# Layer 1 of a hybrid trunk: two heads' queries and keys ahead of the values, a latent-attention head ahead of the differential ones

## Chip, cores and metric

One core of one Trainium2 chip. The metric is the device time of one execution in microseconds (us), the median of several runs; lower is better.

## What is computed

Two layers of one trunk. 256 context tokens and 256 latent tokens of width 1024 share each layer's weights. In each layer the normalised tokens go through one input projection whose columns feed three groups of heads: A, differential attention (4 heads, two softmaxes a head); B, latent attention with low-rank keys and values (4 heads); C, a two-way RWKV-7 recurrence (4 heads, a 64 by 64 state). An output projection, a gated MLP with a width-3 convolution, and residuals follow. Only the latent stream is returned, so layer 1 computes attention outputs for latent tokens alone, which still read the context's keys and values. The part that matters here, cut from the reference:

```python
q1, q2, k1, k2, v = diff_qkv(pa, ang_a)                  # group A, latent tokens
K1 = jnp.concatenate([ck1, k1], axis=1)                  # context keys, then latent keys
V = jnp.concatenate([cv, v], axis=1)
oa = over_query_blocks(lambda a_, b_: diff_attn(a_, b_, K1, K2, V, lam), q1, q2)
qb, kb, vb = mla_qkv(pb, P, ang_b)                       # group B
ob = over_query_blocks(lambda q_: softmax_attn(q_, Kb, Vb), qb)
ocr, S_f, S_b = rwkv7_mix(pcr, zero, zero, P, ctx_out)   # group C, context
orr, _, _ = rwkv7_mix(pr, S_f, S_b, P, True)             # group C, latents, from the context's state

def diff_attn(q1, q2, k1, k2, v, lam):
    p1 = softmax32(jnp.einsum('bqhd,bkhd->bhqk', q1, k1) * scale)
    p2 = softmax32(jnp.einsum('bqhd,bkhd->bhqk', q2, k2) * scale)
    return jnp.einsum('bhqk,bkhe->bqhe', (p1 - lam * p2), v)
```

## The kernel before

Every projection is done with three matmuls for each 128-row piece of the contraction (`mm3`, L276 to L279): weights and activations are split into a high part and a rest. The weights' split is made on chip by `wgroup` (L261): a DMA on SyncE's queue brings 512 KB (`wr..`), ScalarE rounds it to the high part (`wh..`, L269), VectorE takes the difference (`wl..`, L270). In the mixing stage there are 3 buffers for the raw weights, 3 for the high part and 4 for the rest.

The change is in the mixing stage of layer 1, for the latent tokens. `attention` (called with `PLAN1`, L141) writes its steps from a string, one word a step: `b`/`B` the latent-attention projection, `qN` keys and query of differential head N (`diff_project`, L1082: 24 matmuls of 256 columns each for keys and query, then the rotary operation `rope`, L876, on VectorE), `v` the values of all four differential heads for all 512 tokens (`diff_v`, L1048: four weight groups, 96 matmuls of 512 columns into the four PSUM tiles `acc`, then four ScalarE copies, L1059), `pN` queries and keys of latent-attention head N (`prepare`, L988), `yN` latent-attention head N (`head`, L1008), `lN` differential head N, `a` a column chunk of the modulation, `g`/`h` the ends of head pairs. `sN` lets the recurrence's generator (`rwkv_seq`) go N steps further. The recurrence first makes masked scores (matmuls L643 to L646 into PSUM tag `r`, two buffers; VectorE masks each by L648), then inverts a unit triangular matrix by 31 elimination steps on VectorE (a transposition L682, then L695 and L697 in turn, closed by the transposition L700), whose result TensorE uses at L717 and L726; then four steps of the recurrence proper, one for each 64 tokens (L753 to L816).

The words only give the order in which the program is written. A scheduler of the framework then sets each engine's order from the dependencies and its own estimates, and each engine works that order strictly off: what stands behind a waiting instruction waits too. The scheduler may therefore let values' matmuls run between the scores and may move splits of weights far ahead.

## Time and profile before

| | us |
|---|---|
| three timed runs | 1359.21, 1366.96, 1369.14 |
| their median | 1366.96 |
| the profiled execution | 1361.95 |
| its span, first to last instruction | 1360.1 |

Over the whole span TensorE is busy 95%, VectorE 71%, ScalarE 51% and GpSimd 2%; TensorE's mean granted clock is 0.981 of full speed. A busy TensorE is not one at its peak: matmuls are pipelined and the ends shown are modelled, so the starts of successive matmuls tell their price. Busy shares are means over stages with different limits; the rows below are therefore of the stage that is changed, from about 970 to 1130 us of the span.

### The profile page before, as it was taken

How to read it: one execution, taken by the hardware profiler on the slowest of the kernel's cores; microseconds unless marked ns; L12 is line 12 of the kernel's file. 1: busy time of each engine (PE TensorE's matmuls, PEld its weight loads, DVE VectorE, ACT ScalarE, POOL GpSimd, SP SyncE). 2: the span in 40 equal slices, each digit the busy share in tenths (PEclk: the TensorE clock that was granted, in tenths of full speed). 3: DMA queues.
4: the chain of work that ended last, by engine and by line, in shares of the span. 5: the costliest groups of instructions: out<-in, count | busy, mean ns of one | idle time of the engine just before them, and what ended most of it. 6: DMA issues, size and time to landing. Idle time of an engine off the chain costs nothing.

```text
span 1360.1 us, 27958 instructions
## 1 busy us (share of the span) xinstructions
PE 1285.8 (95%) x11208; PEld 1079.1 (79%) x11208; DVE 965.8 (71%) x2438; ACT 696.1 (51%) x1368; POOL 21.1 (2%) x41
## 2 busy tenths in 40 slices
PE   5999999998989999999999999999998997999997
PEld 4787766665777888999999888889865775999996
DVE  3548667657679587866769579587869587777776
ACT  4335244765664554534446555655545654555553
POOL 0001000000000000000000000000100000000000
PEclk9999899997999999999999999999998998999999
DMA  9830265300886565432557446447220048456662
GB/s 323 273 108 16 62 178 183 116 1 2 299 283 189 168 218 170 130 118 78 163 184 224 140 152 206 138 122 214 63 63 1 2 138 265 140 170 202 186 183 81
DMA packets 216531, 202.50 MB, mean 149 GB/s; under 512 B 7825, under 2 KB 175313, under 8 KB 216401
## 3 DMA queue, kind: packets, MB, share of 16 engines
q1 hardware_dynamic: 216400, 200.71, 47.6%
q8 instruction: 88, 1.44, 0.4%
q14 instruction: 43, 0.34, 0.1%
HBM read 198.55 MB, written 2.13 MB: 148 GB/s over the span
## 4 chain that ended last, share of the span: by engine, by line
PE 79%; DVE 13%; ACT 4%; issue 2%; DMA 1%; SPq 0%; POOL 0%; ACTq 0%; DVEq 0%; POOLq 0%
PE g L277 10%; PE g L279 10%; PE g L278 10%; PE acc L277 7%; PE acc L279 7%; PE acc L278 7%; PE r L277 3%; PE r L279 3%; PE r L278 3%; PE acc L906 3%; PE g L1103 2%; PE acc L902 1%; PE r L770 1%; PE r L789 1%; PE acc L322 1%
## 5 line engine op out<-in xcount | busy, mean ns | idle before, releaser
L270 DVE TENSOR_TENSOR wlf<-wrf,whf 128x1024 fp32r<-128x1024 f32 x176 | 214.3, 1220 | 58.8 <-ACT whf L269 37.2
L269 ACT ACTIVATE whf<-wrf 128x1024 fp32r<-128x1024 f32 x176 | 184.6, 1051 | 31.2 <-DMA wrf<-in_ffn_w_up_dram 8.6
L277 PE MATMUL g<-hl,whf 128*128 128x256 f32 x528 | 149.7, 285 | 0.9 <-DVE gv L458 0.8
L278 PE MATMUL g<-hl,whf 128*128 128x256 f32 x528 | 148.9, 284 | 0.0
L279 PE MATMUL g<-hl,wlf 128*128 128x256 f32 x528 | 147.0, 284 | 0.1
L454 ACT ACTIVATE gv<-g,pers 128x256 f32<-128x256 f32 x110 | 61.9, 563 | 155.6 <-PE g L279 154.6
L277 PEld LDWEIGHTS g<-hl,whf 128*128 128x128 f32 x528 | 100.9, 191 | 4.8 <-issue 2.2
L278 PEld LDWEIGHTS g<-hl,whf 128*128 128x128 f32 x528 | 101.0, 191 | 1.9 <-issue 0.3
L277 PE MATMUL g<-hc,whf 128*128 128x256 f32 x352 | 100.6, 286 | 1.6 <-DVE gv L458 0.9
L278 PE MATMUL g<-hc,whf 128*128 128x256 f32 x352 | 100.4, 285 | 0.0
L279 PEld LDWEIGHTS g<-hl,wlf 128*128 128x128 f32 x528 | 99.7, 191 | 1.0 <-issue 0.3
L279 PE MATMUL g<-hc,wlf 128*128 128x256 f32 x352 | 100.0, 285 | 0.0
L457 DVE SCALAR_TENSOR_TENSOR gv<-g,pers,gv 128x255 f32<-128x255 f32 x110 | 52.7, 479 | 65.5 <-ACT gv L454 65.5
L270 DVE TENSOR_TENSOR wlm<-wrm,whm 128x1024 fp32r<-128x1024 f32 (+2 forms) x64 | 71.9, 1132 | 33.3 <-ACT whm L269 19.6
L277 PE MATMUL acc<-whf,at 128*128 128x512 f32 x220 | 87.9, 402 | 0.4 <-ACT ar L344 0.4
L278 PE MATMUL acc<-wlf,at 128*128 128x512 f32 x220 | 87.5, 398 | 0.6 <-DVE wlf L270 0.6
L279 PE MATMUL acc<-whf,at 128*128 128x512 f32 x220 | 86.8, 395 | 0.1
L269 ACT ACTIVATE whm<-wrm 128x1024 fp32r<-128x1024 f32 (+2 forms) x64 | 62.5, 987 | 38.8 <-PE acc L279 17.4
L277 PEld LDWEIGHTS g<-hc,whf 128*128 128x128 f32 x352 | 67.2, 191 | 4.5 <-issue 2.5
L278 PEld LDWEIGHTS g<-hc,whf 128*128 128x128 f32 x352 | 67.2, 191 | 1.5 <-issue 0.2
L279 PEld LDWEIGHTS g<-hc,wlf 128*128 128x128 f32 x352 | 67.1, 191 | 0.4
L895 ACT ACTIVATE pa<-g,pers 128x512 f32<-128x512 f32 (+1 forms) x72 | 44.2, 615 | 32.9 <-DVE pers L894 32.4
(534 smaller groups left out, 3434.4 us busy)
## 6 DMA issues: line engine op xcount, KB each, us to landing
wrf<-in_ffn_w_up_dram SPq DMA_DIRECT2D x110, 512.0 KB
wra<-in_ada_w_dram SPq DMA_DIRECT2D x80, 512.0 KB
wrf<-in_ffn_w_down_dram SPq DMA_DIRECT2D x66, 512.0 KB
wrm<-in_w_in_dram SPq DMA_DIRECT2D x52, 512.0 KB
wro<-in_w_out_dram SPq DMA_DIRECT2D x24, 512.0 KB
wrs<-in_ada_w_dram SPq DMA_DIRECT2D x32, 256.0 KB
gt<-gate SPq DMA_DIRECT2D x6, 512.0 KB
wrm<-in_w_in_dram SPq DMA_DIRECT2D x8, 352.0 KB
```

Of the source, the lines that this page charges most:

```text
L269: S.activation(h[:, :n], raw[:, :n], AF.Copy)
L270: V.tensor_tensor(lo[:, :n], raw[:, :n], h.bitcast(F32)[:, :n], ALU.subtract)
L277: first = TE.matmul(ps, lh[0], rh[0], start=start, stop=False)
L278: TE.matmul(ps, lh[0], rh[1], start=False, stop=False)
L279: TE.matmul(ps, lh[1], rh[0], start=False, stop=stop)
L322: ins = TE.matmul(ps[q * 32 : q * 32 + 32, :], ca[:, k, :], ws[k // 2][:, c0 : c0 + P], start=k == 0, stop=k == KT - 1)
L454: S.activation(o[:, : n * SQ], ps[:, : n * SQ], AF.Identity, scale=wc, bias=bias)
L457: V.scalar_tensor_tensor(o3[:, :, 1:SQ], p3[:, :, 0 : SQ - 1], wp, o3[:, :, 1:SQ], ALU.mult, ALU.add)
L770: chain[s] = TE.matmul(px[eo * 64 : eo * 64 + 64, pd, :], sc[:, pd, eo, 0:64], SV[:, pd, eo, :], start=True, stop=True)
L895: S.activation(pr_[:, :nk], ps[:, :nk], AF.Exp, bias=m, accum_out=sm)
L906: TE.matmul(po[:, :width], pT[:, b * P : (b + 1) * P], vtiles[b], start=(b == 0), stop=(b == nb - 1))
L1103: ins = TE.matmul(ps[:, :nk], qT[:, i, qc : qc + P], kT_[:, :nk], start=True, stop=True)
```

## The change

Layer 1's plan has keys and query of head 1 (`q1`) ahead of the values (`v`) and not behind them, and the latent-attention head `y0` ahead of the differential heads `l1` and `l0`. So that the scheduler does not draw the values' matmuls forward again, the first matmul of each of the values' four tiles (`mm3` returns the first of its three, and `behind` takes it where `k8 == 0`) gets an edge of order alone, without a semaphore, behind the last matmul written before the values, the last one of `q1`'s query. Layer 0 is not touched.

```diff
-    PLAN1 = "b B s15 q0 v p0 s15 q1 l1 l0 s15 y0 g0 p2 p1 q2 y1 p3 y2 s5 l2 q3 y3 a a s99 h a s20 a l3 a g1"
+    PLAN1 = "b B s15 q0 q1 v p0 s15 y0 l1 l0 s15 g0 p2 p1 q2 y1 p3 y2 s5 l2 q3 y3 a a s99 h a s20 a l3 a g1"
...
+    last_mm = [None]
+
+    def behind(ins, first):
+
+        if first is not None:
+            tc.add_manual_dep(
+                ins.ins, first.ins.name,
+                mybir.DependencyInfo(mybir.DependencyClass.NoSync, mybir.DependencyReason.DATA), reason="issue order",
+            )
...
-        TE.matmul(ps, lh[1], rh[0], start=False, stop=stop)
+        last_mm[0] = TE.matmul(ps, lh[1], rh[0], start=False, stop=stop)
...
         pss = [PS(tag) for _ in js]
+        first = last_mm[0]
...
                     ins = mm3(ps, h.tok(k8, j), (wg[0][:, k, :], wg[1][:, k, :]), k8 == 0, k8 == 7)
+                    if l == 1 and k8 == 0:
+                        behind(ins, first)
```

Lines of the changed kernel stand 10 lower than before from `mm3` on, and 13 lower behind `diff_v`. In the names, `g_1457` and the like are PSUM tiles, `hl` latent and `hc` context activations, `whm`/`wlm` the parts of a weight group; equal weight groups carry other numbers in the two kernels.

First place: TensorE, where the values begin. Before: the last matmuls of head 0's query (`g_1457`), then the values' tile `acc_1459`.

```order
L277 MATMUL g_1457_11032<-hl_1340_10255,whm_1455_11028 128x256
L278 MATMUL g_1457_11032<-hl_1340_10255,whm_1455_11028 128x256
L558 MATMUL r_1421_10781<-pers_63,d4_1420_10778 128x2 x3
L279 MATMUL g_1457_11032<-hl_1340_10255,wlm_1456_11029 128x256
L277 MATMUL acc_1459_11063<-whm_1464_11069,hc_994_7676 128x512
L278 MATMUL acc_1459_11063<-wlm_1465_11070,hc_994_7676 128x512
L279 MATMUL acc_1459_11063<-whm_1464_11069,hc_994_7676 128x512
L277 MATMUL acc_1460_11064<-whm_1464_11069,hc_994_7676 128x512
```

Changed: the last matmuls of head 1's query (`g_1467`), then the values' tile `acc_1469`. Ahead of these rows all four pairs of masked scores and the first half of the transposes L681 to L684 have gone.

```order
L288 MATMUL g_1467_11105<-hl_1340_10255,whm_1465_11101 128x256
L289 MATMUL g_1467_11105<-hl_1340_10255,wlm_1466_11102 128x256
L287 MATMUL g_1467_11105<-hl_1340_10255,whm_1465_11101 128x256
L288 MATMUL g_1467_11105<-hl_1340_10255,whm_1465_11101 128x256
L289 MATMUL g_1467_11105<-hl_1340_10255,wlm_1466_11102 128x256
L287 MATMUL acc_1469_11136<-whm_1474_11142,hc_994_7676 128x512
L288 MATMUL acc_1469_11136<-wlm_1475_11143,hc_994_7676 128x512
L289 MATMUL acc_1469_11136<-whm_1474_11142,hc_994_7676 128x512
```

Before, 74 of the values' 96 matmuls stood between and ahead of the scores and 22 behind the first half of the transposes; in the changed order none stands ahead, and all 96 follow in one piece.

Second place: VectorE and ScalarE, ahead of the elimination. VectorE before: two weight rests (of head 1's query and head 2's keys), the rotary operation of `p0`, and the transposition L682 that opens the elimination; head 1's rotary operation comes within it.

```order
L648 TENSOR_TENSOR d4_1439_10916<-r_1441_10918,pers_63 128x4x128
L270 TENSOR_TENSOR wlm_1499_11459<-wrm_1497_11456,whm_1498_11458 128x1024
L270 TENSOR_TENSOR wlm_1562_11904<-wrm_1560_11901,whm_1561_11903 128x1024
L881 STREAM_SHUFFLE sh_1477_11197<-g_1476_11193 32x256
L884 TENSOR_TENSOR sh_1477_11197<-g_1476_11193,pers_63 32x256
L883 TENSOR_TENSOR sh_1477_11197<-sh_1477_11197,pers_63 32x256
L682 STREAM_TRANSPOSE d4_1482_11243<-d4_1429_10840 128x1024
L889 TENSOR_TENSOR bq_1475_11191<-sh_1477_11197 32x256
```

VectorE changed: `wlm_1484` is the values' fourth group, `wlm_1562` and `wlm_1567` are keys and query of head 2, `wlm_1606` keys of head 3; L692 opens the elimination.

```order
L899 TENSOR_TENSOR bq_1485_11264<-sh_1487_11270 32x256
L270 TENSOR_TENSOR wlm_1484_11233<-wrm_1482_11230,whm_1483_11232 128x1024
L270 TENSOR_TENSOR wlm_1562_11904<-wrm_1560_11901,whm_1561_11903 128x1024
L270 TENSOR_TENSOR wlm_1567_11940<-wrm_1565_11937,whm_1566_11939 128x1024
L270 TENSOR_TENSOR wlm_1606_12205<-wrm_1604_12202,whm_1605_12204 128x1024
L692 STREAM_TRANSPOSE d4_1492_11316<-d4_1429_10840 128x1024
L698 COPY d4_1493_11318<-pers_63 128x16 x2
L904 TENSOR_REDUCE pers_63<-g_1503_11494 128x1
```

The elimination now stands behind the rest of a weight group of head 3, two groups further on than before, and the first instruction inside it is a row maximum of `y0`.

ScalarE at the same place, around the four copies of the values (L1059, in the changed kernel L1072). Before: the copies, and right behind them the high part of head 2's keys (`whm_1561`).

```order
L1059 ACTIVATE va_1016_7741<-acc_1459_11063 128x512
L1059 ACTIVATE va_1016_7741<-acc_1460_11064 128x512
L1059 ACTIVATE va_1017_7742<-acc_1461_11065 128x512
L1059 ACTIVATE va_1017_7742<-acc_1462_11066 128x512
L269 ACTIVATE whm_1561_11903<-wrm_1560_11901 128x1024
L1001 ACTIVATE bq_1475_11191<-g_1476_11193 96x256
```

ScalarE changed: the copies, and right behind them the high part of head 3's keys (`whm_1605`), which `wlm_1606` above waits for.

```order
L269 ACTIVATE whm_1561_11903<-wrm_1560_11901 128x1024
L269 ACTIVATE whm_1566_11939<-wrm_1565_11937 128x1024
L1072 ACTIVATE va_1016_7741<-acc_1469_11136 128x512
L1072 ACTIVATE va_1016_7741<-acc_1470_11137 128x512
L1072 ACTIVATE va_1017_7742<-acc_1471_11138 128x512
L1072 ACTIVATE va_1017_7742<-acc_1472_11139 128x512
L269 ACTIVATE whm_1605_12204<-wrm_1604_12202 128x1024
```

The high parts of head 2's two groups moved ahead of the copies, and head 3's took their place behind them.

Third place: TensorE, ahead of the elimination's first use. Before: the last work of `p1` (L997 to L1004), then L717; head 2's projections (`g_1563`) follow.

```order
L906 MATMUL acc_1550_11845<-vb_1015_7740,pa_1547_11833 128x64 x4
L1004 MATMUL g_1559_11897<-bm_1012_7734,bm_1013_7735 64x512
L717 MATMUL r_1485_11317<-d4_1483_11245,d4_1430_10841 32x32 x8
L717 MATMUL r_1485_11317<-d4_1483_11245,d4_1433_10866 32x32 x8
L717 MATMUL r_1485_11317<-d4_1483_11245,d4_1436_10891 32x32 x8
L717 MATMUL r_1485_11317<-d4_1483_11245,d4_1439_10916 32x32 x8
L277 MATMUL g_1563_11907<-hl_1337_10252,whm_1561_11903 128x256
```

Changed: the last matmuls of head 2's query (`g_1568`) and a score matmul of `y1` stand ahead of that use, which is L727 here.

```order
L287 MATMUL g_1568_11943<-hl_1340_10255,whm_1566_11939 128x256
L288 MATMUL g_1568_11943<-hl_1340_10255,whm_1566_11939 128x256
L289 MATMUL g_1568_11943<-hl_1340_10255,wlm_1567_11940 128x256
L1023 MATMUL g_1571_11975<-bq_1556_11886 128x512
L727 MATMUL r_1495_11390<-d4_1493_11318,d4_1430_10841 32x32 x8
```

Head 2's 48 projection matmuls moved from behind L717 to ahead of it.

## Rows read from the trace of the kernel before

**Rows 1.** Busy time by stage: stretch, length, engines (rows), clock, DMA share, GB/s.

```profile
core 0: us, PE busy (x) PEld busy (x) DVE busy (x) ACT busy (x) POOL busy (x), PEclk, DMA share, GB/s
...
974.88:1008.45 33.57, 33.57 (x302) 25.56 (x302) 24.95 (x59) 14.20 (x29) 0.00 (x0) 1.00 0.29 79
...
1012.70:1048.85 36.15, 29.32 (x144) 18.32 (x143) 34.31 (x122) 17.67 (x46) 0.00 (x0) 0.91 0.00 1
...
1048.85:1094.20 45.35, 45.35 (x640) 33.49 (x639) 27.86 (x74) 29.06 (x77) 1.04 (x2) 1.00 0.01 2
...
1094.20:1130.73 36.53, 30.77 (x182) 23.91 (x182) 29.08 (x104) 22.81 (x46) 0.00 (x0) 0.99 0.64 204
```

**Rows 2.** Timeline, TensorE: start us, us, what, [idle before <-releaser].

```profile
974.88 0.40 PE L277 MATMUL acc<-whm,hc 128*128 128x512 f32 x1
...
980.11 0.39 PE L279 MATMUL acc<-whm,hl 128*128 128x512 f32 x1
...
1008.03 0.39 PE L279 MATMUL acc<-whm,hl 128*128 128x512 f32 x1
...
1011.47 0.39 PE L277 MATMUL g<-hl,whm 128*128 128x256 f32 x1
...
1017.21 0.28 PE L279 MATMUL g<-hl,wlm 128*128 128x256 f32 x1
...
1022.54 6.86 PE L1103 MATMUL g<-qk,qz 128*128 128x512 f32 x10 [5.05 <-DVE qz L889]
```

**Rows 3.** Timeline, ScalarE, after the values' last matmul.

```profile
1006.41 2.64 ACT L1059 ACTIVATE va<-acc 128x512 f32<-128x512 f32 x4 [2.10 <-PE acc L279]
...
1009.08 1.06 ACT L269 ACTIVATE whm<-wrm 128x1024 fp32r<-128x1024 f32 x1
```

**Rows 4.** Timeline, VectorE, around the scores and the elimination.

```profile
980.95 2.35 DVE L270 TENSOR_TENSOR wlm<-wrm,whm 128x1024 fp32r<-128x1024 f32 x2
...
983.22 0.87 DVE L574 SCALAR_TENSOR_TENSOR d<-rk,pers,r 128x256 f32<-128x256 f32 x2
...
990.57 0.68 DVE L624 TENSOR_TENSOR rk<-r,rk 128x512 f32<-128x512 f32 x1
...
1000.69 1.29 DVE L648 TENSOR_TENSOR d<-r,pers 128x512 f32<-128x512 f32 x2 [0.90 <-PE r L644]
...
1010.16 1.23 DVE L270 TENSOR_TENSOR wlm<-wrm,whm 128x1024 fp32r<-128x1024 f32 x1 [7.05 <-ACT whm L269]
...
1012.70 2.09 DVE L682 STREAM_TRANSPOSE d<-d 128x1024 f32<-128x1024 f32 x1
...
1047.81 1.04 DVE L700 STREAM_TRANSPOSE d<-d 128x512 f32<-128x512 f32 x1
```

**Rows 5.** Lines, VectorE, 1012.7 to 1048.85: line, shapes, count | busy us, mean ns.

```profile
L695 DVE TENSOR_TENSOR d<-d,d 128x126 f32<-128x126 f32 (+22 forms) x31 | 7.8, 252 | 0.4
...
L697 DVE TENSOR_TENSOR d<-d,d 128x126 f32<-128x126 f32 (+22 forms) x31 | 7.8, 251 | 0.4
...
L270 DVE TENSOR_TENSOR wlm<-wrm,whm 128x1024 fp32r<-128x1024 f32 x2 | 2.4, 1216 | 0.0
...
L881 DVE STREAM_SHUFFLE sh<-g 128x256 f32<-128x256 f32 (+1 forms) x3 | 1.3, 442 | 0.1
...
L883 DVE TENSOR_TENSOR sh<-sh,pers 128x256 f32<-128x256 f32 (+1 forms) x2 | 0.8, 422 | 0.0
```

**Rows 6.** Timeline, TensorE, the four steps of the recurrence.

```profile
1049.14 1.98 PE L717 MATMUL r<-d,d 32*32 32x32 f32 x64
...
1054.28 0.27 PE L753 MATMUL r<-pers,rk 64*64 64x64 f32 x1
...
1093.73 0.45 PE L816 MATMUL r<-std,d 128*64 128x64 f32 x8
```

**Rows 7.** Lines, TensorE, 1048.85 to 1094.2.

```profile
L277 PE MATMUL g<-hl,whm 128*128 128x256 f32 x17 | 5.3, 311 | 0.0
...
L1124 PE MATMUL acc<-pers,oh 128*128 128x128 f32 x4 | 0.7, 286 | 0.0
```

**Rows 8.** Busy time, 10 us from 1020: columns as in rows 1.

```profile
1020.00:1030.00 10.00, 6.86 (x10) 2.76 (x10) 9.00 (x29) 2.33 (x6) 0.00 (x0) 0.66 0.00 1
```

## The prediction

> **What bounds the kernel now.** I read four views in this order: busy time by stage, the timelines of the three engines through the changed stage, VectorE's and TensorE's costliest lines in two of its stretches, and busy time in slices of 10 us. The reader should see three different limits in one stage.
>
> From 974.88 to 1008.45 TensorE has no gap: 33.57 us busy of 33.57 [rows 1]. The values' matmuls fill whatever time the masked scores leave, and the scores' chain runs on VectorE beside them [rows 4]. So the values cost little beyond their own 96 issues.
>
> From 1012.70 to 1048.85 VectorE is the limit: 34.31 of 36.15 us busy, while TensorE has 29.32 at a granted clock of 0.91 [rows 1]. This is the elimination, from L682 to L700 [rows 4]. Its own 62 operations are only 15.6 us [rows 5]; the rest is other VectorE work that stands between them.
>
> From 1048.85 to 1094.20 TensorE is busy for the whole 45.35 us [rows 1]: the recurrence's four steps take 1054.28 to 1093.73 and a bit, about 39.9 us or 10.0 a step [rows 6], and projections of other heads stand between their links [rows 7].
>
> What joins these is a chain: last value matmul ends at 1008.45, four copies on ScalarE end at 1009.05 [rows 2, 3], the split L269 takes 1.06 behind them [rows 3], VectorE, idle for 7.05 us and waiting for exactly that split, takes the rest L270 at 1010.16 and only then opens the elimination at 1012.70 [rows 4]. The elimination itself needs nothing of the values. It is late because it stands on VectorE behind a weight rest whose high part stands on ScalarE behind the values' copies. The changed order keeps this link (second place in the order above), so the question is when the values end.
>
> **The values' end.** Before, 74 of the 96 lay among the scores; now all 96 come behind the scores, all of head 1's 48 matmuls, and the first transposes. First the scores. The two weight rests at 980.95 (2.35 us) [rows 4] give way to one rotary part of three operations, about 3 x 0.42 = 1.2 [rows 5], so the chain of preparations on VectorE is 1.15 earlier: its last row, which ended at 990.57 + 0.68 = 991.25 [rows 4], ends near 990.1. Behind it VectorE has eight masks (1.29 for two [rows 4], so 0.65 each, 5.2) and three weight rests (1.22 each [rows 5], 3.6), with 0.4 for the first matmul before a mask: 999.3. Then TensorE makes the first transposes, about 1.0 (an estimate: half the 1.98 of L717's 64 matmuls as small as these [rows 6]) and the last eight of the query's matmuls, 8 x 0.12 = 1.0, where 0.12 is (1017.21 - 1011.47) over 47 intervals [rows 2]. With a link of 0.2 the values start near 1001.5. They start 1.5 earlier if those matmuls run beneath the last mask, and 2.7 later if three pairs of masks each wait 0.90 for their matmuls as one did [rows 4].
>
> The values' spacing is (980.11 - 974.88) / 23 = 0.227 us [rows 2], so 96 take 21.8 and end near 1023.3. Copies 0.6, split 1.06, rest 1.22, links 0.2: the elimination opens at 1026.4 instead of 1012.70, **+13.7** (bounds +12.2 and +16.4).
>
> A cross-check by TensorE's work alone: with no gap the stretch would end 48 x 0.12 = 5.8 us later, at 1014.2. That it ends at 1023.3 means some 9 us of gaps among the scores, which the values no longer fill; VectorE's masks and rests set the pace there.
>
> **Inside the elimination.** Out of it go about ten rotary operations (head 1's nine and one of `p0`), 10 x 0.43 = 4.3 [rows 5], and, net, one weight rest, 1.2. Into it come the rotary operations of `p1` and of head 2's keys, eight of 0.42, 3.4, a normalising product and a query's rest of 0.7 each (estimates by the 0.68 of the 512-column row in [rows 4]). Sum **-0.6**: 35.5 us in place of 36.15. The reordering of `y0`, `l1` and `l0` adds and removes no operation; their order within a stretch that VectorE bounds costs nothing as long as TensorE ends first. It should: 29.32 busy at 0.91 is 26.7 us of full clock, head 1's 48 matmuls go out, head 2's 48 come in. The elimination then closes near 1026.4 + 35.5 = 1061.9, **+13.1**.
>
> **After it.** Head 2's 48 matmuls and the four of L1124 (0.66 by their row, 4 x 0.286 = 1.1 if not overlapped [rows 7]) now stand ahead of the first use of the elimination's result: 48 x 0.12 + 0.66 = 6.4 us less in a stretch where TensorE has no gap [rows 1]. They are paid for beneath the elimination, where TensorE waits anyway (5.05 us in one place [rows 2]). What is late next is the recurrence's own links, which these matmuls covered in the first step: TensorE, VectorE and ScalarE hand on five times a step, and VectorE is busy 27.86 of 45.35 and ScalarE 29.06 [rows 1], 61 and 64%. I take 1.4 us of exposed links (about two gaps of the 0.7 that small operations take), so **-5.0**. Bounds: 0, if the links are what takes the 10 us a step, and -6.4. The stretch 1094.20 to 1130.73 [rows 1] has the same instructions in the same order: 0.
>
> Moved DMAs: the weights' loads keep their order with the plan's words, and DMA has a 29% share among the scores and none in the elimination [rows 1], so I cost them at nothing; if one comes late, it is within the +16.4.
>
> Sum: +13.7 - 0.6 - 5.0 = **+8.1**. The profiled execution took 1361.95, so 1370.0; the median of the runs shown is 1366.96, so 1375.1. I do not know which of the two a new series lies nearer to and take the middle of the bases, 1364.5: **1372.5 us**. One per cent, about what a measurement of this kernel can tell from no change, is 13.7 us, so +8 counts as no change.
>
> **Rivals.**
>
> A, everything is given back (other side). TensorE's work is the same in both kernels and it is busy 95% of the span; if the recurrence's steps are limited only by the work between their links, the steps could shrink from 10.0 to 10.0 - 13.1/4 = 6.7 us, the point from which this decides, and the lateness is gone at the end: 1364.5 or slightly below. For it: TensorE is without a gap there, and the last stretch has 36.53 - 30.77 = 5.8 us free [rows 1]. Against: only 6.4 us of work have moved out; the rest of the filling still stands between the links.
>
> B, nothing is given back. A gapless TensorE in that stretch can be modelled ends: the links (TensorE to VectorE to ScalarE and back) take 10 us a step and the projections lie beside them free. Then +13.1: 1377.6. For it: head 2's 48 matmuls at 0.12 are 5.8 us of issue, but the rows call their lines busy 311 ns each [rows 7], so busy time overstates. Against: 640 matmuls in 45.35 us is one per 71 ns, with 48 at 120 among them. The Trainium skill, "Perfetto Trace Analysis", section "Identifying the Most-Contended Engine", says that matmul busy time is a poor measure, since matmuls are pipelined, and that the busy share of weight loads is a better one. By it this stretch is 33.49 / 45.35 = 74% full [rows 1], the moved 6.4 us might have been free, and the time would be B's.
>
> C, the clock. From 1020 to 1030 the granted clock is 0.66 with TensorE busy 6.86 us of 10 [rows 8], after a wait of 5.05 [rows 2]; the levels are 1.2 and 2.4 GHz. If the changed elimination, whose heads wait for VectorE even more often, runs at that clock throughout, TensorE needs (26.7 + 0.7) / 0.66 = 41.5 us where VectorE needs 35.5, and the first use comes 6.0 later: +14.1, 1378.6. It decides from 27.4 / 35.5 = 0.77 downwards. Against: the mean over the whole elimination was 0.91 [rows 1]. The Trainium skill, "TensorE: Matmul & The Clock Gate", Part 1, says the lower clock is the default and that sustained activity releases it; the row agrees in that the fall comes after the wait.
>
> That the change does not do what it says is excluded by the order shown above.
>
> **How the numbers follow.** Forecast 0.56, with a range of its own from 1366 to 1378 (the bounds of the start, of the give-back in part, and the 2.6 us on either side between the two bases); A 0.13, B 0.19, C 0.12. The range reaches from a little below A to a little above C: 1361.5 to 1381.5. Faster by over 1% (below 1353.3) needs A and another 11 us: 0.05. Slower by over 1% (above 1380.6) is half of C, a quarter of B and the upper end of the forecast: 0.20. Within 1%: 0.75.
>
> **What would show it.** In the profile of the changed kernel: the values in one piece from about 1001.5 to 1023.3 with VectorE waiting for ScalarE's split just before the elimination; the elimination's first transposition (L692) near 1026.4, its last near 1061; the first use (L727) within 1 us of it; four steps that end near 1102. If the elimination opens before 1020, or the values start before the masks end, the first step of the sum is wrong. If the first step of the recurrence still takes 10 us or more, the give-back is; if the granted clock in the elimination is below 0.77, C has come.

## The result, and the profile after

The changed kernel takes 1374.05 us (median of 13 runs, 1368.01 to 1385.81) against 1364.83 us for the kernel before, measured again beside it (13 runs, 1359.04 to 1375.47). The ratio is 1.0081, 95% interval 1.0059 to 1.0104: slower by 11 us, or 0.8%, and inside the bound of 1% that the forecast set for "no change", though clear of zero. The profiled execution has a span of 1372.2 us, 12.1 more than before. The one of the changed kernel (1374.04 us) is at its median, the one of before (1361.95) is 2.9 us below that kernel's median, so a part of the 12.1 belongs to the two executions and not to the change.

The stage after, to be read against [rows 1]. The columns are stretch, length, then busy time and instructions of TensorE, its weight loads, VectorE, ScalarE and GpSimd, the granted clock, DMA share and GB/s:

```profile
core 0: us, PE busy (x) PEld busy (x) DVE busy (x) ACT busy (x) POOL busy (x), PEclk, DMA share, GB/s
974.00:1004.28 30.28, 23.74 (x277) 20.12 (x276) 26.11 (x69) 12.73 (x28) 0.00 (x0) 0.83 0.19 53
1004.28:1026.54 22.26, 22.26 (x101) 18.22 (x101) 8.26 (x15) 6.68 (x9) 0.11 (x1) 1.00 0.26 71
1029.29:1064.48 35.19, 29.20 (x158) 19.06 (x156) 33.97 (x123) 19.17 (x49) 0.00 (x0) 1.00 0.00 1
1064.48:1107.91 43.43, 42.01 (x597) 29.86 (x597) 23.24 (x64) 27.15 (x74) 1.03 (x2) 0.92 0.01 2
1107.91:1142.44 34.53, 28.82 (x170) 22.41 (x169) 27.81 (x99) 21.77 (x46) 0.00 (x0) 0.99 0.65 214
```

What was one stretch before, 974.88 to 1008.45 with TensorE at 33.57 of 33.57, has fallen apart into two. In the first, the scores, TensorE works 23.74 of 30.28 us at a clock of 0.83; in the second, the values in one piece, VectorE works 8.26 of 22.26. The overlap of the two engines is what is gone.

The two executions do not start the stage at the same moment. The same wait of TensorE just ahead of it, in an order that the two kernels share, stands in the kernel before at

```profile
967.15 0.33 PE L962 MATMUL acc<-pers,pa 128*128 128x128 f32 x1 [1.84 <-DVE pa L230]
```

and in the changed kernel at

```profile
968.76 0.33 PE L972 MATMUL acc<-pers,pa 128*128 128x128 f32 x1 [1.82 <-DVE pa L230]
```

so 1.6 of the 12.1 us have nothing to do with the change. Below, times "from that wait" are differences to 967.15 and 968.76, and in other kernels to the same row.

TensorE's timeline of the changed kernel, to be read against [rows 2, 6] (start us, us, what, idle before and what ended it):

```profile
982.69 1.16 PE L579 MATMUL r<-pers,d 128*128 128x128 f32 x8 [2.93 <-DVE d L223]
...
987.96 0.47 PE L653 MATMUL r<-d,d 64*64 64x128 f32 x1 [2.22 <-DVE d L625]
...
990.64 0.47 PE L653 MATMUL r<-d,d 64*64 64x128 f32 x1 [1.25 <-DVE d L625]
...
1004.59 0.40 PE L287 MATMUL acc<-whm,hc 128*128 128x512 f32 x1
...
1026.15 0.39 PE L289 MATMUL acc<-whm,hl 128*128 128x512 f32 x1
...
1064.53 1.98 PE L727 MATMUL r<-d,d 32*32 32x32 f32 x64 [1.23 <-DVE d L710]
...
1067.39 0.28 PE L736 MATMUL r<-d,d 32*32 32x32 f32 x2 [0.88 <-DVE d L223]
```

Three gaps of 2.93, 2.22 and 1.25 us open ahead of and among the scores, where before there was none; the values run from 1004.59 to 1026.54 without one, and two new gaps stand at the first use of the elimination's result. ScalarE's copies and split behind the values, to be read against [rows 3]:

```profile
1024.54 2.64 ACT L1072 ACTIVATE va<-acc 128x512 f32<-128x512 f32 x4 [8.01 <-PE acc L289]
...
1027.07 1.05 ACT L269 ACTIVATE whm<-wrm 128x1024 fp32r<-128x1024 f32 x1
```

VectorE around the elimination, against [rows 4]:

```profile
992.12 0.69 DVE L658 TENSOR_TENSOR d<-r,pers 128x512 f32<-128x512 f32 x1 [0.19 <-PE r L654]
...
997.93 1.34 DVE L658 TENSOR_TENSOR d<-r,pers 128x512 f32<-128x512 f32 x2 [1.32 <-PE r L656]
...
1002.46 0.69 DVE L658 TENSOR_TENSOR d<-r,pers 128x512 f32<-128x512 f32 x1 [0.85 <-PE r L656]
...
1028.15 1.23 DVE L270 TENSOR_TENSOR wlm<-wrm,whm 128x1024 fp32r<-128x1024 f32 x1 [10.36 <-ACT whm L269]
...
1029.29 1.95 DVE L692 STREAM_TRANSPOSE d<-d 128x1024 f32<-128x1024 f32 x1
...
1063.45 1.03 DVE L710 STREAM_TRANSPOSE d<-d 128x512 f32<-128x512 f32 x1
```

The chain is the one that was read before the change, only later: last value matmul, copies, split (L269), the rest L270 for which VectorE waits 10.36 us, and then the opening transposition. What was not foreseen is in the clock (same columns as above, changed kernel):

```profile
979.00:984.00 5.00, 2.07 (x17) 1.84 (x16) 4.69 (x19) 2.01 (x3) 0.00 (x0) 1.00 0.00 0
984.00:989.00 5.00, 2.74 (x16) 1.43 (x14) 5.00 (x13) 0.38 (x1) 0.00 (x0) 0.89 0.00 0
989.00:994.00 5.00, 3.70 (x44) 2.80 (x40) 4.81 (x12) 0.62 (x2) 0.00 (x0) 0.50 0.60 158
994.00:999.00 5.00, 4.95 (x46) 4.27 (x42) 3.68 (x6) 1.56 (x6) 0.00 (x0) 0.59 0.52 160
999.00:1004.00 5.00, 5.00 (x122) 4.50 (x121) 3.30 (x5) 2.91 (x10) 0.00 (x0) 1.00 0.00 0
...
1062.00:1067.00 5.00, 3.28 (x70) 2.29 (x68) 4.23 (x10) 1.75 (x5) 0.39 (x1) 0.94 0.02 3
1067.00:1072.00 5.00, 4.36 (x82) 3.38 (x82) 4.13 (x15) 4.01 (x12) 0.65 (x2) 0.50 0.01 2
```

TensorE stands at 1.2 GHz (0.50) behind both groups of gaps: in the middle of the scores, and where the recurrence begins. The Trainium skill, "TensorE: Matmul & The Clock Gate", Part 1, says that the clock is released by sustained activity and falls without it; the rows agree as to where it fell.

### The profile page after: what moved, and what is told of

It is laid out like the page before. It is cut to its first block, busy times and chain, and to the rows that moved or that the text cites. A ratio compares the mean times of both kernels' runs of the same rounds, so it can differ in the third digit from the quotient of the medians.

```text
span 1372.2 us, 27970 instructions
## 1 busy us (share of the span) xinstructions
PE 1290.1 (94%) x11208; PEld 1085.2 (79%) x11208; DVE 965.9 (70%) x2438; ACT 695.8 (51%) x1368; POOL 21.1 (2%) x41
## 4 chain that ended last, share of the span: by engine, by line
PE 74%; DVE 17%; ACT 5%; DMA 2%; issue 2%; SPq 0%; POOL 0%; DVEq 0%; ACTq 0%; POOLq 0%
PE g L287 10%; PE g L289 9%; PE g L288 9%; PE acc L287 6%; PE acc L288 6%; PE acc L289 6%; PE r L287 3%; PE r L289 3%; PE r L288 3%; PE acc L916 2%; PE g L1116 2%; DVE wlf L270 2%; PE acc L912 1%; PE r L799 1%; DMA wrf<-in_ffn_w_up_dram 1%
## 5 line engine op out<-in xcount | busy, mean ns | idle before, releaser
L270 DVE TENSOR_TENSOR wlf<-wrf,whf 128x1024 fp32r<-128x1024 f32 x176 | 214.6, 1222 | 59.6 <-ACT whf L269 35.7
L269 ACT ACTIVATE whf<-wrf 128x1024 fp32r<-128x1024 f32 x176 | 184.6, 1051 | 32.3 <-DMA wrf<-in_ffn_w_up_dram 11.6
L270 DVE TENSOR_TENSOR wlm<-wrm,whm 128x1024 fp32r<-128x1024 f32 (+2 forms) x64 | 72.1, 1134 | 36.9 <-ACT whm L269 27.2
L269 ACT ACTIVATE whm<-wrm 128x1024 fp32r<-128x1024 f32 (+2 forms) x64 | 62.5, 987 | 43.5 <-PE acc L289 19.3
L904 DVE TENSOR_REDUCE pers<-g 128x1 f32<-128x512 f32 (+1 forms) x72 | 42.7, 599 | 28.1 <-PE g L1116 16.3
```

Of the source, the lines that this page charges most:

```text
L269: S.activation(h[:, :n], raw[:, :n], AF.Copy)
L270: V.tensor_tensor(lo[:, :n], raw[:, :n], h.bitcast(F32)[:, :n], ALU.subtract)
L904: V.tensor_reduce(m, ps[:, :nk], axis=AX.X, op=ALU.max, negate=True)
```

## Experiments

All ratios are to the kernel before, run beside them; the changed kernel's is 1.0081 (1.0059 to 1.0104).

### Without the edge, and with the old order of heads

The first kernel (no_edge) has the new words without the edge:

```diff
-                    if l == 1 and k8 == 0:
-                        behind(ins, first)
+                    pass
```

> The changed plan without the edge of order; the issue order then has all four pairs of masked scores among the values again, while queries and keys of head 1 stay ahead. Theory (the values in one piece leave TensorE with gaps among the scores, and the elimination follows the values' end): the values end near 1014 (1008.45 of before + 48 x 0.12 of head 1), the elimination opens near 1017, TensorE has no gap among the scores and its granted clock stays at 1.00 there; the time falls from 1374 to about 1364, within 3 us of before. Rival (the words of the plan cost the time, by the order of the heads and of the weights' loads, and the edge only fixes what the scheduler would do): 1372 or more.

Measured: ratio 1.0122 (1.0069 to 1.0175), median 1379.7. The rival's 1372 or more came. The theory was wrong in its premise: this kernel's order has only 4 of the values' matmuls ahead of the scores and 92 behind them. The scheduler does not draw the values forward here with or without the edge, most likely since their weights now come behind head 1's two groups. So the edge is not what costs the time: without it the loss is there too, and nothing separates the two kernels, whose intervals overlap. The profile shows how much the clock can add, by 5 us from 990:

```profile
990.00:995.00 5.00, 1.64 (x12) 0.91 (x12) 5.00 (x17) 0.23 (x1) 0.00 (x0) 0.70 0.11 14
995.00:1000.00 5.00, 4.96 (x45) 3.92 (x42) 4.77 (x9) 1.52 (x5) 0.00 (x0) 0.50 0.82 243
1000.00:1005.00 5.00, 5.00 (x45) 4.22 (x46) 3.11 (x4) 1.56 (x6) 0.00 (x0) 0.50 0.21 62
1005.00:1010.00 5.00, 5.00 (x62) 4.45 (x60) 1.59 (x3) 1.23 (x4) 0.00 (x0) 0.50 0.00 0
1010.00:1015.00 5.00, 4.91 (x70) 4.60 (x64) 0.69 (x1) 2.53 (x5) 0.00 (x0) 0.50 0.01 3
```

In this execution the clock stayed at 0.50 for twenty microseconds, from 995 to 1015.

The second kernel (q1_edge) is the changed one with `y0` back behind `l1` and `l0`, the third (y0_only) the kernel before with only `y0` moved ahead:

```diff
-    PLAN1 = "b B s15 q0 q1 v p0 s15 y0 l1 l0 s15 g0 p2 p1 q2 y1 p3 y2 s5 l2 q3 y3 a a s99 h a s20 a l3 a g1"
+    PLAN1 = "b B s15 q0 q1 v p0 s15 l1 l0 s15 y0 g0 p2 p1 q2 y1 p3 y2 s5 l2 q3 y3 a a s99 h a s20 a l3 a g1"
```

> The changed kernel with the latent-attention head y0 back behind the differential heads l1 and l0; edge and head 1 ahead of the values as changed. Theory (the order of heads within the elimination costs nothing, VectorE bounds it): the elimination opens at 1029 and takes 35 us as in the changed kernel, 1374 plus or minus 2. Rival (the moved head lengthens the elimination or leaves gaps on TensorE behind the values): 1371 or less; rival of the other sign (the moved head covers VectorE's waits for head 1): 1377 or more.

```diff
-    PLAN1 = "b B s15 q0 v p0 s15 q1 l1 l0 s15 y0 g0 p2 p1 q2 y1 p3 y2 s5 l2 q3 y3 a a s99 h a s20 a l3 a g1"
+    PLAN1 = "b B s15 q0 v p0 s15 q1 y0 l1 l0 s15 g0 p2 p1 q2 y1 p3 y2 s5 l2 q3 y3 a a s99 h a s20 a l3 a g1"
```

> The kernel before with only the latent-attention head y0 ahead of l1 and l0; head 1 stays behind the values, no edge. Theory (all of the loss comes from head 1 ahead of the values): as before, ratio 1.000 plus or minus 0.003; the elimination opens at 1012.7. Rival (the order of the heads is part of the loss): ratio 1.004 or more.

Measured: 1.0158 (1.0094 to 1.0222), median 1387.13, and 1.0008 (0.9986 to 1.0029). `y0` alone changes nothing, as the theory had it. The first of the two lies where its rival of the other sign was put, at 1377 or more. Its interval overlaps the changed kernel's, though, and its four runs have mean clocks from 0.965 to 0.974, so whether `y0` ahead of the differential heads helps once head 1 stands in front is not shown. The loss is there in all of these kernels that have head 1 ahead of all the values, and not in the one that has only `y0` moved.

### The elimination early

In early_after, edges of order on VectorE, put into the changed kernel, hold the rests behind step 27 of the elimination and the row maxima behind step 24:

```diff
+        rest = V.tensor_tensor(lo[:, :n], raw[:, :n], h.bitcast(F32)[:, :n], ALU.subtract)
+        if hold[0] is not None:
+            behind(rest, hold[0])
...
+            if l == 1 and s == LAT and si == 27:
+                hold[0] = step
+            if l == 1 and s == LAT and si == 24:
+                hold.append(step)
...
+        if len(hold) == 2:
+            behind(top, hold[1])
```

> The changed kernel with edges of order alone on VectorE: the weights' rests of heads 2 and 3 and of later groups stand behind step 27 of the elimination, the heads' row maxima behind step 24. Theory (the elimination is late only because it stands behind a rest that waits for the values' copies): it opens near 1012, closes near 1034 instead of 1064.5, and the recurrence then runs with the heads' TensorE work between its links; the time falls by 10 us or more, to 1364 or less. Rival (TensorE's work and the gaps among the scores are what was lost, the late elimination lies beside work that has to be done anyway): 1371 to 1375.

Measured: 1.0135 (1.0085 to 1.0184), median 1380.63. The opening transposition on VectorE, and the first work of a head on TensorE, in this kernel:

```profile
1022.14 2.10 DVE L694 STREAM_TRANSPOSE d<-d 128x1024 f32<-128x1024 f32 x1 [9.69 <-PE acc L290]
...
1040.98 1.12 PE L920 MATMUL acc<-pers,pa 128*128 128x128 f32 x4 [9.06 <-ACT pa L913]
```

That is longer than both expectations. The theory falls in two places. Without the rest ahead of it, the transposition waits 9.69 us for a matmul of the values all the same: in the built program its output tile lies at the same address as the rest of the values' third weight group, and it opens when the last matmul that reads that rest (L290) is done. And although the elimination then closes 14.5 us earlier from the wait ahead of the stage (1048.66 + 1.05 - 968.50 = 81.2 against 1064.48 - 968.76 = 95.7), the recurrence ends no earlier (1107.74 - 968.50 = 139.2 against 1107.91 - 968.76 = 139.2): TensorE stood idle 9.06 us for the held maxima, and the heads' work came into the recurrence instead, which took 58.0 us with TensorE busy for 57.1. In this kernel an early end of the elimination did not shorten the stage. Since the hold itself made TensorE wait, the run does not show what an early elimination without such a wait would be worth.

### Head 2's matmuls back behind the first use

The changed kernel with the first matmuls of head 2's two projections held by an edge (q2_held):

```diff
+                        if held[1]:
+                            behind(ins, held[0])
...
+        if l == 1 and s == LAT:
+            held[0] = last_727
...
+                held[1] = l == 1 and n == 2
```

> The changed kernel with the 48 matmuls of head 2's projections held behind the first use of the elimination's result, where they stood before the change; with them some four VectorE operations and a rest leave the elimination, which closes some 3 us earlier. Theory (what the moved matmuls gave back was eaten: exposed links and the lower clock they leave at the recurrence's start): no gap and clock 1.00 from the first use on, as before the change; time 1371 to 1373. Rival (moving them out of the recurrence does give 5 us, something else is lost later): first use 3 earlier, recurrence 5 longer: 1376.

Measured: 1.0164 (1.0115 to 1.0212), median 1384.72, slower than the changed kernel, intervals apart, and outside both expectations. TensorE ahead of the first use (L729 here):

```profile
1057.05 1.09 PE L1141 MATMUL acc<-pers,oh 128*128 128x128 f32 x4 [5.79 <-DVE d L707]
1059.27 2.01 PE L729 MATMUL r<-d,d 32*32 32x32 f32 x64 [1.13 <-DVE d L712]
```

With the 48 matmuls gone TensorE waits 5.79 us at the end of the elimination, and the clock is 0.50 for the recurrence's start. The elimination is 2.5 us shorter than in the changed kernel (32.7 against 35.2) and the recurrence 5.0 longer (48.4 against 43.4, at a mean clock of 0.88 against 0.92), as the rival had it. Their place beneath the elimination was worth having, then; the term of the sum has the right sign. The larger part of the loss in this kernel's profile lies behind the recurrence, 43.9 against 34.5 us, and was expected by neither side.

### TensorE kept busy in the gaps

Extra matmuls of constants into a tile that the real ones overwrite (warm_scores):

```diff
+    def warm(ps, n, wait=None, first=None):
+
+        for i in range(n):
+            ins = TE.matmul(ps, ident, C("mask"), start=True, stop=True)
...
+                if l == 1 and s == LAT and c == 0:
+                    warm(pe[:, 256:512], (6, 3)[pr], (w2, w1)[pr])
```

> The changed kernel with nine extra TensorE matmuls of 256 columns (constants, overwritten by the real ones) in two of TensorE's gaps among the masked scores: six ahead of the first score, three ahead of the fifth. Nothing else moves. Theory (after those gaps TensorE is granted its lower level, 1.2 GHz, and that is what makes the values start and end late): the granted clock from 984 to 1000 stays near 1.00 instead of falling to 0.5, the waits of VectorE for scores go, the values start 3 us earlier, and the time falls by 3 to 8 us against the changed kernel, to 1366 to 1371 by the first series. Rival (VectorE alone sets the pace of the scores; the clock does not matter there): the nine matmuls change nothing or cost up to 2 us, 1374 to 1376.

and in the second kernel (warm_both) also

```diff
+            warm(pz[:, 0:256], 4, w3)
...
+            warm(pt[:, 0:256], 2, None, last_727)
```

> As warm_scores, and four such matmuls ahead of the first use of the elimination's result and two behind it, where the changed kernel waits 1.23 and 0.88 us and shows a clock of 0.50 from 1067 to 1072. Theory: the first step of the recurrence keeps the clock at 1.00 and is 2 to 3 us shorter than in warm_scores: 1364 to 1368 by the first series, within 3 us of before. Rival (the links alone set that step): as warm_scores plus or minus 1.

Measured: 1.0058 (1.0031 to 1.0084), median 1372.03, and 1.0062 (1.0040 to 1.0085), median 1372.48. The first lies between what its two sides expected, and the second is as the first, which is what its rival expected. The clock ahead of and among the scores, first kernel:

```profile
979.00:984.00 5.00, 3.55 (x14) 3.13 (x14) 3.78 (x14) 0.00 (x0) 0.00 (x0) 0.66 0.00 0
984.00:989.00 5.00, 4.58 (x26) 3.14 (x25) 5.00 (x15) 0.38 (x1) 0.00 (x0) 1.00 0.00 0
989.00:994.00 5.00, 3.70 (x54) 2.92 (x52) 4.74 (x10) 0.95 (x4) 0.00 (x0) 1.00 0.80 222
994.00:999.00 5.00, 5.00 (x89) 4.39 (x92) 4.88 (x7) 2.79 (x10) 0.00 (x0) 1.00 0.35 96
```

and at the first use, second kernel:

```profile
1063.00:1068.00 5.00, 4.85 (x134) 3.90 (x134) 4.23 (x16) 3.34 (x11) 1.04 (x2) 1.00 0.02 5
1068.00:1073.00 5.00, 4.14 (x67) 2.75 (x61) 2.87 (x9) 4.61 (x12) 0.00 (x0) 1.00 0.00 0
```

The clock follows the gaps, as the theory had it: 1.00 in both places that the extra matmuls fill, and 0.66 from 979 to 984, behind the first gap, which they leave open. The first and the last mask on VectorE in the first kernel (there L671):

```profile
990.86 0.69 DVE L671 TENSOR_TENSOR d<-r,pers 128x512 f32<-128x512 f32 x1 [0.26 <-PE r L667]
...
999.49 0.69 DVE L671 TENSOR_TENSOR d<-r,pers 128x512 f32<-128x512 f32 x1 [0.61 <-PE r L669]
```

The clock's price in the profiled pair is small. First mask to last takes 999.49 - 990.86 = 8.6 us in the warm kernel against 1002.46 - 992.12 = 10.3 in the changed one, so 1.7 us among the scores. Counted from the wait ahead of the stage (966.51 and 967.41 in these two kernels) the values start 0.7 and 1.6 us earlier than in the changed kernel, not 3 (35.1 and 34.2 against 35.8), and the elimination closes no earlier (96.6 and 95.7 against 95.7): its length is 36.7 and 36.8 us, where the changed kernel has 35.2. From the first use to the recurrence's end the second kernel takes 42.7 us, the changed one 43.4. Against the changed kernel the ratios are some 3 us lower and the medians 2 us or less, but the intervals overlap, and the 1.9 us by which the first kernel's profiled span is shorter (1370.3) lie ahead of the stage. A gain in time is not shown. Most of the loss is not the clock in these two places: with it at 1.00 in both, the second kernel still loses 0.4 to 0.85%.

### The values in two parts

The changed order of heads, but three of the values' four weight groups written ahead of head 1 and the rest behind it (split3), or two ahead (split2, with `v2`), without the edge:

```diff
-    PLAN1 = "b B s15 q0 q1 v p0 s15 y0 l1 l0 s15 g0 p2 p1 q2 y1 p3 y2 s5 l2 q3 y3 a a s99 h a s20 a l3 a g1"
+    PLAN1 = "b B s15 q0 v3 q1 v p0 s15 y0 l1 l0 s15 g0 p2 p1 q2 y1 p3 y2 s5 l2 q3 y3 a a s99 h a s20 a l3 a g1"
...
-                    last[0] = run(diff_v(l, hboth, va, range(4), "acc"))
...
+                    if n:
+                        values[0].step(n)
+                    else:
+                        last[0] = values[0].run()
```

> The changed order of heads with three of the values' four weight groups written ahead of head 1 and the last behind it, without the edge; the issue order then has 72 of the values' 96 matmuls ahead of and among the masked scores again, all 48 of head 1 behind the scores, then the last 24. Theory (head 1 ahead costs only because the values no longer fill TensorE among the scores): TensorE has no gap there, the values end 48 x 0.12 = 5.8 us later than before, near 1014, the elimination opens near 1017 to 1018 and the recurrence gives some 4 us of that back: ratio to before 1.000, 0.998 to 1.003. Rival (head 1 ahead of the values' end costs in itself, since the elimination waits for that end): ratio 1.006 or more.

> As split3 with two groups ahead: 48 of the values' matmuls stand in one piece ahead of the scores, head 1's 48 partly among them, and the last 48 values behind. Theory (what matters is that TensorE has work among the scores, whichever it is): the scores start up to 5 us later behind that piece, TensorE has only head 1's 48 matmuls beneath them, so some gaps remain; ratio between split3's and the changed kernel's, 1.002 to 1.006. Rival (no difference from the changed kernel): 1.008 or more.

Measured: 1.0001 (0.9977 to 1.0025) with three groups ahead, and 0.9994 (0.9971 to 1.0017) with two. TensorE among the scores, and VectorE's opening of the elimination, with three groups ahead:

```profile
994.00:999.00 5.00, 5.00 (x39) 3.14 (x35) 4.17 (x10) 0.56 (x2) 0.00 (x0) 1.00 0.59 157
999.00:1004.00 5.00, 5.00 (x75) 3.72 (x74) 3.53 (x5) 1.90 (x7) 0.00 (x0) 1.00 0.34 98
```

```profile
1020.84 1.23 DVE L270 TENSOR_TENSOR wlm<-wrm,whm 128x1024 fp32r<-128x1024 f32 x1 [4.05 <-ACT whm L269]
1023.36 1.91 DVE L692 STREAM_TRANSPOSE d<-d 128x1024 f32<-128x1024 f32 x1
```

This is the decisive pair for the order: head 1 ahead of the values' end costs nothing by itself. It is ahead here too, and the elimination opens late, 1023.36 - 970.74 (the wait ahead of the stage in this kernel) = 52.6 us behind that wait against 1012.70 - 967.15 = 45.6 before, 7.1 later; it still stands behind the rest that waits for the copies. But TensorE has no gap among the scores, and by the many runs the loss is gone. With two groups ahead it is gone as well; that this order would keep a part of the loss was wrong.

TensorE's account of the whole stage, from the wait ahead of it to the end of the stretch behind the recurrence, in the kernel before, the changed one, three groups ahead, two groups ahead, and y0_only:

```profile
967.15:1130.73 163.58, 151.00 (x1398) 110.90 (x1398) 125.55 (x383) 93.47 (x217) 2.75 (x5) 0.98 0.22 66
...
968.76:1142.44 173.68, 153.91 (x1398) 115.60 (x1398) 125.30 (x382) 93.74 (x218) 2.74 (x5) 0.95 0.20 62
...
970.74:1138.49 167.75, 154.36 (x1397) 113.72 (x1397) 125.91 (x382) 93.83 (x218) 2.78 (x5) 0.96 0.22 67
...
966.58:1135.55 168.97, 155.26 (x1397) 115.29 (x1398) 124.86 (x382) 93.30 (x218) 2.78 (x5) 0.95 0.22 67
...
963.86:1134.82 170.96, 156.77 (x1397) 116.50 (x1397) 125.03 (x383) 93.83 (x218) 2.75 (x5) 0.94 0.21 64
```

Length less busy time is TensorE's idle time: 12.6 us before, 19.8 changed, 13.4 and 13.7 with the values in two parts, 14.2 in y0_only. The lengths themselves are less to be trusted: y0_only, whose time over many runs is that of the kernel before, has a stage 7.4 us longer in its one profiled execution, at a clock of 0.94 against 0.98.

What the pair does not separate is the gaps from the lateness that they cause: without the gaps the elimination is also only 7.1 us late, where it is 15.0 late in the changed kernel.

### Two trials at a faster version

The kernel before with `p0` written later and head 2's rests held behind step 14 (ob2), and split2 with the same rests held behind step 10 (split2_hold). The first against the kernel before:

```diff
-    PLAN1 = "b B s15 q0 v p0 s15 q1 l1 l0 s15 y0 g0 p2 p1 q2 y1 p3 y2 s5 l2 q3 y3 a a s99 h a s20 a l3 a g1"
+    PLAN1 = "b B s15 q0 v s15 p0 q1 l1 l0 s15 y0 g0 p2 p1 q2 y1 p3 y2 s5 l2 q3 y3 a a s99 h a s20 a l3 a g1"
...
+        if hold[0] is not None and hold[-1] == 'on':
+            behind(rest, hold[0])
...
+            if l == 1 and s == LAT and si == 14:
+                hold[0] = step
...
+                if l == 1 and n == 2:
+                    hold.append('on')
```

> A trial at a version better than both: the kernel before, with the queries and keys of p0 written behind the second stretch of the recurrence, and the weights' rests of head 2 and later groups held by an edge of order behind step 14 of the elimination, so that the elimination's opening transposition stands right behind head 1's query rest and not behind a rest that waits for the values' copies. Theory: it opens near 1003 instead of 1012.7, waits once near 1009 for p0, and closes 4 to 5 us earlier; TensorE has the heads' work left then, so the time falls by 2 to 4 us, ratio 0.997 to 0.998. Rival (TensorE's work bounds the stage already): ratio 1.000; rival of the other sign (TensorE gets a gap at the first use and a lower clock behind it): above 1.002.

and the second against split2, with the same hold:

```diff
+            if l == 1 and s == LAT and si == 10:
+                hold[0] = step
```

> split2 with the weights' rests of head 2 and later groups held by an edge of order behind step 10 of the elimination, so that the rotary operation of p0 and the opening transposition no longer stand behind a rest that waits for the values' copies. In split2 VectorE waited 7.89 us for that rest, and TensorE 3.50 us for p0 behind the values. Theory (that wait is the last one that still comes from the values' end): the opening comes some 3 us earlier against the values' end, TensorE's 3.50 us go, ratio to before 0.996 to 0.999. Rival (TensorE's and VectorE's work bounds the stage, as early_after and ob2 suggest): ratio 0.999 to 1.002.

Measured: 1.0039 (1.0014 to 1.0064) and 1.0082 (1.0051 to 1.0112): both slower than the kernel that they start from. The first is what its rival of the other sign expected, the second is outside both of its expectations. In the first the transposition waited 4.05 us for a matmul of the values, and the clock was 0.50 at the recurrence's start (a stretch of 5 us):

```profile
1055.00:1060.00 5.00, 5.00 (x89) 4.35 (x88) 4.25 (x18) 4.68 (x14) 0.30 (x1) 0.50 0.01 3
```

In the second the held rests came to lie inside the elimination, TensorE waited 2.83 and 2.11 us at its end, and the mean clock of the recurrence was 0.82. In these two trials, what was pulled out from ahead of the elimination was paid inside and behind it. No version was found that is shown to be faster than the kernel before.

## Why the prediction was right

The forecast was 1372.5 us, +8.1, within 1%; measured are +11.0 us by the ratio, 1374.05 as the median. The chain that it named, with values, copies, split, rest and elimination in turn, is the one that ran. That the number came so near owes something to luck: the new median of the kernel before, 1364.83, fell on the middle of the two bases, and a give-back taken 3.1 us too large was made good by 2.0 us from a stretch that was put at nothing. Term by term, from the wait ahead of the stage:

| term of the sum | forecast | measured |
|---|---|---|
| opening of the elimination | +13.7 | 60.53 - 45.55 = +15.0 |
| length of the elimination | -0.6 | 35.19 - 36.15 = -1.0 |
| recurrence, from its close to its end | -5.0 | 43.43 - 45.33 = -1.9 |
| the stretch behind it | 0 | 34.53 - 36.55 = -2.0 |
| the rest of the program | 0 | +0.4 |
| sum | +8.1 | +10.5 |

(The recurrence of before ends at 1094.18; the stretch behind it ends at 1130.73 and 1142.44.) With the 1.6 us ahead of the stage this is the 12.1 by which the spans differ. The column is one execution against one, and the rows of y0_only above show how far a single one can be off.

**The values' end.** The chain was right step by step: the values in one piece, 0.227 us apart ((1026.15 - 1004.59) / 95), copies, split, rest, transposition. Its start was mis-sized: 1001.5 was forecast, 1004.59 measured. Of these 3.1 us 1.6 is the later start of the stage, and 2.2 stand in the masks: from the first one's start to the last one's end they take 992.12 to 1003.15, 11.0 us where 8.8 were forecast, since VectorE waits 1.32 and 0.85 us there for TensorE, which the sum had only in its bound of 2.7. The transposes and last matmuls behind them took 0.8 less than forecast. Of the 2.2 the warm kernels take away 1.7. The cross-check by TensorE's work had said that some 9 us of gaps would open. TensorE was idle for 6.5 us from 974 to 1004.28, and the work that it did there ran at a mean clock of 0.83: gaps were counted as idle time alone, and not as a reason for a lower clock.

**What the elimination cost.** The prediction named the late elimination as the way in which the loss reaches the end. Two runs bear on that: in early_after it closed 14.5 us earlier and nothing was won, but TensorE was made to wait elsewhere; in the kernel with three groups ahead it opened 7.1 us late and nothing was lost over many runs. Lateness of the elimination is thus not by itself the loss. TensorE's idle time over the stage goes with the loss in the changed kernel and the two with the values in parts: 7.2 us more than before where the time is lost, some 1 us more where it is not. That agrees with what rival A argued from, TensorE's work, which comes out at nothing lost only when no gap opens. Whether lateness beyond what the recurrence and the stretch behind it can take up would cost time without any gap among the scores, no run shows.

**The give-back.** -5.0 was placed where most of head 2's matmuls had stood, at the recurrence's first use and first step. This is the term that the runs do not bear out. Before, the first step ran from 1054.28 [rows 6] to the start of the second, in this row:

```profile
1063.90 0.27 PE L753 MATMUL r<-pers,rk 64*64 64x64 f32 x1
```

and in the changed kernel from the first of these rows to the second:

```profile
1069.76 0.36 PE L763 MATMUL r<-pers,rk 64*64 64x64 f32 x1
...
1079.44 0.27 PE L763 MATMUL r<-pers,rk 64*64 64x64 f32 x1
```

It takes 9.7 us where it took 9.6, and the time from the elimination's close to its start is 5.3 us where it was 5.4. Exposed waits of 1.23, 0.88 and 0.25 us, where 1.4 in all was taken, and a clock of 0.50 behind them took up what left. The recurrence's 1.9 us come from its last step, 1099.56 to 1107.91 or 8.4 us where it was 10.2 (1084.03 to 1094.18); why that one shrank is not shown. A further 2.0 come from the stretch behind it, taken as 0. The sum of both, -3.9, is nearer the term than either, by luck. In the second warm kernel, with the clock at 1.00 there, the recurrence takes 42.8 us, 2.6 less than before: half of the term. The Trainium skill, "Perfetto Trace Analysis", section "Identifying the Most-Contended Engine", had been weighed against it: a stretch whose weight loads are 74% busy need not be full. That the stretch of [rows 1] without a gap gave only 1.9 us for 6.4 us of work taken out agrees with that more than with the term.

**The rivals.** A and B did not come: neither all nor nothing was given back. B's mechanism, links that set the length of a step with the projections free beside them, fits the first step, which had matmuls taken out and did not shrink; but it ran in part at the lower clock, and in the second warm kernel, at 1.00, it took 9.3 us. C came in another place. In the elimination, where it was looked for, the clock was 1.00 against 0.91 before; it was low among the scores and at the first use. The edge of order, which the prediction did not price, costs nothing that could be measured, and neither does `y0` ahead of the differential heads in the order of before.

What stays open: how much of the loss is the clock over many executions (the two warm kernels put it near 2 to 3 us, with intervals that overlap), and how the loss divides between TensorE's gaps and the late elimination that follows from them.

## What to carry to other kernels

Before moving independent work out from between the links of another engine's chain, ask what TensorE does there afterwards: here 74 matmuls that looked free were the filling, and without them TensorE was idle for 7.2 us more over the stage. Check a forecast made along a chain by the sum of an engine's work and gaps over the stage; here it told of the gaps before anything ran. Read where a term comes out and not only its sum: the give-back came, in part, in other places than forecast. If work has to go ahead, leave a part of the filling in its place: the same move with half of the values left ahead of head 1 costs nothing that could be measured (0.9971 to 1.0017).

## What the runs showed that was not expected

The changed kernel's runs spread from 1368.01 to 1385.81 us, and the time goes with each run's mean granted clock: 0.981 in the shortest, 0.966 in the longest, a slope of 11.8 us for 0.01 over the 13 runs. In its profiled execution the changed kernel met a clock near 0.50 for some ten microseconds among the scores; no_edge, with nearly the same order, met 0.50 for twenty (its rows above, with TensorE busy 4.91 to 5.00 of each 5.00 us).

Tiles of different names can share memory in this program: in early_after the elimination's first tile lies where a rest of the values' weights lay, in ob2 where context activations lay that the values' matmuls read. An edge of order that frees the engine therefore does not free the work (waits of 9.69 and 4.05 us on a values' matmul in the two kernels).
